# One weight array for the first two products of an encoder layer, and transposes four half steps later

## The chip, the cores and the metric

The kernel runs on one core of a Trainium2 chip. The metric is the device time of one execution in microseconds (us). The core has five engines that run side by side, each through its own list of instructions: TensorE (PE, matrix products, results go to PSUM banks), VectorE (DVE), ScalarE (ACT), GpSimd (POOL) and SyncE (SP), which here issues nearly all DMAs.

## The reference, cut to what matters

A trunk of two layers on 256 tokens of width 1024, in float32. The first layer, the even one, has two groups of attention heads behind one input projection:

```python
def even_mixer(xn, w_in, rpb, q_norm, w_uq, kv_norm, w_ukv, w_o, cos_r, sin_r):
    hcat = xn @ w_in                      # 1024 x (3*512 + 256 + 128 + 32)
    a_qkv = hcat[..., :o0]                # queries, keys, values of neighbourhood attention
    out_a = neighbourhood_attention(...)
    c_q = rms_norm(hcat[..., o0:o1], q_norm)      # latent inputs: 256
    c_kv = rms_norm(hcat[..., o1:o2], kv_norm)    # and 128 columns,
    k_pe = apply_rope(hcat[..., o2:], ...)        # and 32 columns
    q = (c_q @ w_uq) ...; kv = (c_kv @ w_ukv) ...
    out_b = dense_attention(q, k, v, ...)
    return jnp.concatenate([out_a, out_b], axis=-1) @ w_o
```

`xn` is the RMS norm of `x`. After each mixer comes an MLP, then the odd layer, its MLP, and a final norm.

## The kernel before, in words

Activations lie feature first: `x` is 8 tiles of 128 features by 256 tokens. Precision is kept by splitting each operand of a product into a rounded upper part and the rest: a weight tile `raw` becomes `whi` (ACT, a cast, line 167) and `wlo` (DVE, a subtraction, line 168), `x` becomes `xh` and `xl` (`prepare`), and each product is three matmuls (`mm3`, lines 171 to 173: upper by upper, then the two cross terms).

Weights are loaded in the order of the list `specs` into four raw buffers, and split in four pieces each (`split_piece`). `weight()` hands out the next split weight and first issues loads and splits some weights ahead.

The even layer starts with two products that have the tokens as rows: the latent inputs, 416 columns from `w_c` (banks `pc`, one for each half of the tokens), and the values, 512 columns from `w_v` (`pv`). Before the change `c_product` runs inside the loop over the 8 tiles of `x`; the values follow behind it (`v_steps`), with `rstd(s)` (the norm's factor: two small matmuls at line 223, DVE at 225, POOL at 231) among them. The norm's factor is applied to results, not to `x`: `c_tail` (lines 487 to 508) squares and normalizes the latent inputs in 2 + 1 parts with ACT, POOL and DVE in turn, rotates 32 columns (`kpe`), and returns a step that transposes the result on PE (line 506) and splits it into `cT`; `v_out` scales the values.

Then come queries and keys of neighbourhood attention, four weights `w_qk` of two heads each. `qk_steps(c)` gives four half steps of 12 matmuls; its last multiplies the result by `both` (the norm's factor as a row, made by `as_row`, line 258) into `q32`, and splits that into `qk_h` and `qk_l`. From the second weight on these half steps form the list `main`, into which the attention's steps (`side`: scores at line 180, transposes of probabilities, mixing) are woven by their costs; the first scores need `qk_h` and `qk_l` of the first weight.

Inside `manual_schedule` the three engines keep the written order. Elsewhere a scheduler orders the instructions when the program is built; each engine then runs its list in that order, and an instruction that waits for a semaphore holds up all behind it on its engine. `issue_after` keeps a block's instructions behind a given one.

Of the kernel before, what the change touches and what calls it, by code (L numbers as in the profile page):

```python
# [20 lines left out]
ENG = mybir.EngineType  # L21
# [9 lines left out]
NEG = -1e30  # L31
EPS = 1e-6

MLA_SCALE = (64 + 32) ** -0.5
WCH = 2048
WBUFS = 3
# [8 lines left out]
def trunk(ctx, tc, a, out):  # L45
# [23 lines left out]
    def bank(tag):  # L69
        return ps.tile([P, 512], F32, tag=tag, name=tag)  # L70
# [28 lines left out]
    def plan(name, n):  # L99
        for j in range(a[name].shape[0]):  # L100
            specs.append((a[name][j], n))
# [7 lines left out]
        for j in (14, 15):  # L109
            specs.append((a["w2"][layer, j], WCH))  # L110

    plan("w_c", 4 * 416)
    plan("w_v", 4 * 512)
    plan("w_qk", WCH)
    plan("w_ukv", 1024)
    plan("w_uq", 2 * 768)
# [12 lines left out]
    def load_weight(pieces=1, before=lambda i: None):  # L129
        j = state["loaded"]  # L130
        src, n = specs[j]
        raw = wraw.tile([P, WCH], F32, tag="raw", name="raw")
        for i in range(pieces):
            c = cut(j, i, pieces)
            before(i)
            nc.sync.dma_start(raw[:, c], src[:, c])
        parts[j] = [raw, None, None]
        state["loaded"] = j + 1
# [31 lines left out]
    def mm3(o, sh, sl, mh, ml, first, last):  # L170
        nc.tensor.matmul(o, sh, mh, start=first, stop=False)  # L171
        nc.tensor.matmul(o, sh, ml, start=False, stop=False)  # L172
        nc.tensor.matmul(o, sl, mh, start=False, stop=last)  # L173
# [17 lines left out]
    def tok(t):  # L191
        return slice(t * P, (t + 1) * P)
# [254 lines left out]

    def even(ep):
        xT = xh, xl = half_tile(act, "xh", 2), half_tile(act, "xl", 2)
        for j in range(2):  # L450
            load_weight(4, lambda i: nc.sync.dma_start(x[:, 4 * j + i, :], a["x"][:, 4 * j + i, :]))
        load_weight(2)
        load_weight()
        both = ep.tile([P, 2, T], F32, name="both")

        cosr = ep.tile([P, NT, 32], F32, name="cosr")
# [22 lines left out]
        kpe = ep.tile([P, NT, 32], F32, name="kpe")  # L479
        vna = ep.tile([P, NT, 512], F32, name="vna")  # L480

        def c_product(pc, wc, k, t):
            wh, wl = wc
            ws = slice((k % 4) * 416, (k % 4) * 416 + 416)
            mm3(pc[:, 0:416], xh[:, k, tok(t)], xl[:, k, tok(t)], wh[:, ws], wl[:, ws], k == 0, k == KT - 1)

        def c_tail(t, pc):
            rt = column(r, t)
# [18 lines left out]
                split(cT_h[:, 0:3, tok(t)], cT_l[:, 0:3, tok(t)], pt[:, 0:384].rearrange("p (k n) -> p k n", k=3))  # L507
            return step

        def v_steps(t):  # L510
            hold = []

            def step(ks):
                if not hold:
                    hold.append(bank("acc"))
                for k in ks:
                    if t == 0 and k % 4 == 0:
                        wv.append(weight())
                    wh, wl = wv[k // 4]
                    ws = slice((k % 4) * 512, (k % 4) * 512 + 512)  # L520
                    mm3(hold[0], xh[:, k, tok(t)], xl[:, k, tok(t)], wh[:, ws], wl[:, ws], k == 0, k == KT - 1)
                return hold[0]
            return step

        def v_out(t, pv):
            nc.scalar.activation(vna[:, t, :], pv, AF.Copy, scale=column(r, t))

        wc, wv = [], []
        pc = [bank("acc") for _ in range(NT)]
        s = sum_tile()  # L530
        with tc.manual_schedule(engines={ENG.PE, ENG.Activation, ENG.DVE}):
            for k in range(KT):
                upper, lower = prepare(k, 0, xT)
                upper()
                lower()
                split_piece()
                if k % 4 == 0:
                    wc.append(parts[k // 4][1:])
                for t in range(NT):
                    c_product(pc[t], wc[k // 4], k, t)  # L540
                if k % 2:
                    add_squares(k // 2, s)
            state["used"] = 2
            del parts[0], parts[1]
            ins = [split_piece() for _ in range(WPARTS)][-1]
        with tc.issue_after(ins[0]), tc.issue_after(ins[1]):
            with tc.manual_schedule(engines={ENG.PE, ENG.Activation, ENG.DVE}):
                v0, v1 = v_steps(0), v_steps(1)
                v0(range(4))
                small_loads()  # L550
                r = rstd(s)
                dg = [diagonal(r, t) for t in range(NT)]
                v1(range(4))
                pv = v0(range(4, KT))
                turn_c = [c_tail(0, pc[0])]
                v_out(0, pv)
                turn_c.append(c_tail(1, pc[1]))
                v_out(1, v1(range(4, KT)))


        qk = {}
# [157 lines left out]
        nc.scalar.mul(both[:, 0, :], row, HD ** -0.5)  # L719
        nc.scalar.copy(both[:, 1, :], row)  # L720
        run_all(first[3:])
        turn_c[0]()


        accs, wo = [], {}
        main = [(1.31, f) for c in range(1, 4) for f in qk_steps(c)]
        main.insert(1, (0, turn_c[1]))
        i = lambda t, h: 2 * t + h
        for h in range(2):
            main += [(.65, kg[i(0, h)]), (.98, ug[i(0, h)]), (.43, kt[i(0, h)]), (.65, kg[i(1, h)]), (.43, ut[i(0, h)]),  # L730
# [219 lines left out]
def _layout(i):  # L950
    f = np.ascontiguousarray
    w = i["ev_w_in"][0]
    d = {"x": f(i["x"][0][ORDER].T.reshape(KT, P, T).transpose(1, 0, 2))}
    d["w_c"] = f(w[:, 1536:].reshape(2, 4, P, 416).transpose(0, 2, 1, 3).reshape(2, P, -1))
    d["w_qk"] = f(w[:, :1024].reshape(KT, P, 2, 4, P).transpose(3, 1, 0, 2, 4).reshape(4, P, -1))
    d["w_v"] = f(w[:, 1024:1536].reshape(2, 4, P, 512).transpose(0, 2, 1, 3).reshape(2, P, -1))
    d["w_uq"] = f(i["ev_w_uq"][0].reshape(1, 2, P, 768).transpose(0, 2, 1, 3).reshape(1, P, -1))
    d["w_ukv"] = f(i["ev_w_ukv"][0].reshape(1, P, 1024))
    d["w_oe"] = f(i["ev_w_o"][0].reshape(4, 2, P, D).transpose(0, 2, 1, 3).reshape(4, P, -1))
# [44 lines left out]
```

## Time and profile before

| what | value |
|---|---|
| median of 3 runs | 767.98 us (767.9 to 768.18) |
| the profiled execution's own time | 768.55 us |
| its span, first to last instruction | 766.7 us |
| PE busy | 757.2 us, 99% of the span |
| DVE, ACT busy | 500.8 us (65%), 507.5 us (66%) |

A matmul's record shows its start and a modelled end; matmuls overlap, so the distance from start to start is what one costs on PE. A row of the timeline gives start, duration, engine, line, operation, what it writes and reads, how many records are merged, and in brackets how long its engine was idle before it and what ended that.

### The profile page before, as it was taken

What the parts mean: (1) busy time and instruction counts of PE and PEld (TensorE: products, weight loads), DVE (VectorE), ACT (ScalarE), POOL (GpSimd) and SP (SyncE); (2) the same over time, 40 slices, a digit from 0 to 9 for tenths busy, and PEclk for the clock granted to TensorE, in tenths of its full rate; (3) what the DMA queues carried; (4) which work ended last, traced back from release to release, by engine and by line L of the source; (5) the groups of instructions that cost most, each with busy time, mean ns of one, the idle gap of its engine ahead of it and who ended that gap; (6) DMA issues with size and microseconds to landing.
All of it is one profiled execution on the core that took longest, in us unless ns stands there. A gap on an engine that the chain in (4) does not pass through costs nothing.

```text
span 766.7 us, 14611 instructions
## 1 busy us (share of the span) xinstructions
PE 757.2 (99%) x5898; PEld 716.6 (93%) x5898; DVE 500.8 (65%) x1028; ACT 507.5 (66%) x1078; POOL 9.5 (1%) x22
## 2 busy tenths in 40 slices
PE   8999999999999999999999999999999999999996
PEld 5998999999999999999999999999999899899895
DVE  6788858655555557877667676767749555555564
ACT  6788967444444445888988989989857454454541
POOL 0100000000000001000000000000000000000000
PEclk9999999999999999999999999999999999999999
DMA  8763334555555444643452534435454554554501
GB/s 282 302 227 132 111 110 167 173 212 167 172 212 168 170 186 149 207 160 125 167 183 104 203 110 176 159 120 184 165 194 164 172 214 165 172 213 168 178 40 55
DMA packets 22819, 129.13 MB, mean 168 GB/s; under 512 B 2913, under 2 KB 5473, under 8 KB 9825
## 3 DMA queue, kind: packets, MB, share of 16 engines
q1 hardware_dynamic: 22464, 127.94, 47.5%
q8 instruction: 46, 0.75, 0.4%
q10 hardware_dynamic: 288, 0.28, 0.1%
q14 instruction: 21, 0.16, 0.1%
HBM read 127.16 MB, written 1.05 MB: 167 GB/s over the span
## 4 chain that ended last, share of the span: by engine, by line
PE 89%; ACT 5%; DVE 2%; issue 2%; DMA 1%; SPq 0%; POOLq 0%; POOL 0%
PE acc L171 19%; PE acc L172 18%; PE acc L173 18%; PE w L171 9%; PE w L172 9%; PE w L173 9%; PE w L180 1%; DMA raw<-in_w_c 1%; ACT whi L167 1%; PE w L859 1%; PE w L683 1%; PE w L843 1%; PE w L697 1%; DVE wlo L168 1%; PE acc L868 1%
## 5 line engine op out<-in xcount | busy, mean ns | idle before, releaser
L168 DVE TENSOR_TENSOR wlo<-raw,whi 128x512 fp32r<-128x512 f32 (+3 forms) x488 | 307.5, 663 | 165.6 <-ACT whi L167 164.6
L167 ACT CAST whi<-raw 128x512 fp32r<-128x512 f32 (+3 forms) x488 | 268.7, 600 | 201.9 <-issue 173.3
L172 PE MATMUL w<-xl,whi 128*128 128x256 f32 x528 | 149.1, 282 | 0.0
L173 PE MATMUL w<-xh,wlo 128*128 128x256 f32 x528 | 149.0, 282 | 0.0
L171 PE MATMUL w<-xh,whi 128*128 128x256 f32 x528 | 148.8, 282 | 0.0
L171 PE MATMUL acc<-xh,whi 128*128 128x256 f32 x432 | 125.2, 290 | 0.0
L173 PE MATMUL acc<-xh,wlo 128*128 128x256 f32 x432 | 121.9, 282 | 0.0
L172 PE MATMUL acc<-xl,whi 128*128 128x256 f32 x432 | 121.8, 282 | 0.0
L171 PEld LDWEIGHTS w<-xh,whi 128*128 128x128 f32 x528 | 99.6, 189 | 0.6
L172 PEld LDWEIGHTS w<-xl,whi 128*128 128x128 f32 x528 | 99.3, 188 | 0.5
L173 PEld LDWEIGHTS w<-xh,wlo 128*128 128x128 f32 x528 | 99.5, 188 | 0.0
L171 PEld LDWEIGHTS acc<-xh,whi 128*128 128x128 f32 x432 | 81.4, 188 | 2.4 <-issue 1.4
L172 PEld LDWEIGHTS acc<-xl,whi 128*128 128x128 f32 x432 | 81.6, 189 | 0.0
L173 PEld LDWEIGHTS acc<-xh,wlo 128*128 128x128 f32 x432 | 81.2, 188 | 0.0
L171 PE MATMUL acc<-hh,whi 128*128 128x256 f32 x256 | 72.6, 284 | 0.0
L172 PE MATMUL acc<-hl,whi 128*128 128x256 f32 x256 | 72.4, 283 | 0.0
L173 PE MATMUL acc<-hh,wlo 128*128 128x256 f32 x256 | 72.4, 283 | 0.0
L171 PE MATMUL acc<-whi,xh 128*128 128x384 f32 (+2 forms) x160 | 57.5, 359 | 0.9 <-ACT whi L167 0.9
L172 PE MATMUL acc<-wlo,xh 128*128 128x384 f32 (+2 forms) x160 | 55.8, 349 | 0.4 <-DVE wlo L168 0.4
L173 PE MATMUL acc<-whi,xl 128*128 128x384 f32 (+2 forms) x160 | 54.9, 343 | 0.0
L171 PEld LDWEIGHTS acc<-hh,whi 128*128 128x128 f32 x256 | 49.1, 192 | 0.0
L173 PEld LDWEIGHTS acc<-hh,wlo 128*128 128x128 f32 x256 | 49.1, 192 | 0.0
(202 smaller groups left out, 1289.9 us busy)
## 6 DMA issues: line engine op xcount, KB each, us to landing
raw<-in_w SPq DMA_DIRECT2D x64, 1024.0 KB, 4.8
raw<-in_w_oqk SPq DMA_DIRECT2D x24, 1024.0 KB, 4.8
raw<-in_w_ov SPq DMA_DIRECT2D x16, 768.0 KB, 4.3
raw<-in_w_qk SPq DMA_DIRECT2D x4, 1024.0 KB, 10.5
raw<-in_w_oe SPq DMA_DIRECT2D x4, 1024.0 KB, 5.2
raw<-in_w_oo SPq DMA_DIRECT2D x4, 1024.0 KB, 4.8
bias<-in_rpb SPq DMA_DIRECT2D x8, 256.0 KB, 4.0
raw<-in_w_c SPq DMA_DIRECT2D x8, 208.0 KB, 4.7
```

Source lines behind the costliest of these rows:

```text
L167: a = nc.scalar.copy(hi, src).ins
L168: return a, (eng or nc.vector).tensor_tensor(lo, src, hi.bitcast(F32), op=ALU.subtract).ins
L171: nc.tensor.matmul(o, sh, mh, start=first, stop=False)
L172: nc.tensor.matmul(o, sh, ml, start=False, stop=False)
L173: nc.tensor.matmul(o, sl, mh, start=False, stop=last)
L180: nc.tensor.matmul(o[j], y[pb, 0, ts], z[pb, 1, :], start=n == 0, stop=n == 2)
L683: nc.tensor.transpose(pt[:, b * P:(b + 1) * P], pp[:, b // 2, (b % 2) * P:(b % 2 + 1) * P], ident)
L697: nc.tensor.matmul(pvo[64 * j:64 * j + 64, 0:P], v[:, kk, h * 64:(h + 1) * 64], pts[:, 2 * j + kk, :], start=kk == 0, stop=kk == NT - 1)
L843: nc.tensor.matmul(ss[j][rows, T:T + P], d["q12"][:, j, i * P + 64 * c:i * P + 64 * c + 64], d["k12"][:, j, 2 * i + c, :], start=True, sto ...
L859: nc.tensor.transpose(pt[:, b * P:(b + 1) * P], pp[:, b * P:(b + 1) * P], ident)
L868: nc.tensor.matmul(pvo[cs, 0:P], d["v0"][:, kk, cs], turned[i, j][:, kk, :], start=kk == 0, stop=False)
```

## The change

`w_c` and `w_v` become one array, `w_cv`, with 416 + 512 columns for each tile of 128 features; a raw buffer holds two tiles' worth (1856 columns). It is loaded in pieces: the first buffer in four of 464 columns (with the first two tiles of `x` between them), the other three in two pieces of 928 columns, each behind its tile of `x`. As each tile of `x` arrives, both products are done with it, for both halves of the tokens: 6 matmuls of 416 and 6 of 512 columns. `rstd`, `c_tail` and `v_out` stand behind all of them, and the split of the next weight (`w_qk`, first of four) stands in the program behind those. The two transposing steps `turn_c`, before run after the first weight's half steps and one half step later, stand behind the four half steps of the second weight.

```diff
-    plan("w_c", 4 * 416)
-    plan("w_v", 4 * 512)
+    plan("w_cv", 2 * CV)
...
-        for j in range(2):
-            load_weight(4, lambda i: nc.sync.dma_start(x[:, 4 * j + i, :], a["x"][:, 4 * j + i, :]))
+        def load_x(k):
+            nc.sync.dma_start(x[:, k, :], a["x"][:, k, :])
+
+        load_weight(4, lambda i: load_x(i // 2) if i % 2 == 0 else None)
+        for j in range(1, 4):
+            load_weight(2, lambda i: load_x(2 * j + i))
         load_weight(2)
-        load_weight()
...
-        def c_product(pc, wc, k, t):
-            wh, wl = wc
-            ws = slice((k % 4) * 416, (k % 4) * 416 + 416)
-            mm3(pc[:, 0:416], xh[:, k, tok(t)], xl[:, k, tok(t)], wh[:, ws], wl[:, ws], k == 0, k == KT - 1)
+        def first_products(o, w, k, t, c0, n):
+            ws = slice((k % 2) * CV + c0, (k % 2) * CV + c0 + n)
+            mm3(o[:, 0:n], xh[:, k, tok(t)], xl[:, k, tok(t)], w[0][:, ws], w[1][:, ws], k == 0, k == KT - 1)
...
-        wc, wv = [], []
-        pc = [bank("acc") for _ in range(NT)]
+        pc, pv = [bank("acc") for _ in range(NT)], [bank("acc") for _ in range(NT)]
         s = sum_tile()
         with tc.manual_schedule(engines={ENG.PE, ENG.Activation, ENG.DVE}):
             for k in range(KT):
                 upper, lower = prepare(k, 0, xT)
                 upper()
                 lower()
-                split_piece()
-                if k % 4 == 0:
-                    wc.append(parts[k // 4][1:])
+                for _ in range(WPARTS // 2):
+                    ins = split_piece()
+                w = parts[k // 2][1:]
                 for t in range(NT):
-                    c_product(pc[t], wc[k // 4], k, t)
+                    first_products(pc[t], w, k, t, 0, 416)
+                for t in range(NT):
+                    first_products(pv[t], w, k, t, 416, 512)
                 if k % 2:
                     add_squares(k // 2, s)
-            state["used"] = 2
-            del parts[0], parts[1]
-            ins = [split_piece() for _ in range(WPARTS)][-1]
+                    state["used"] += 1
+                    del parts[k // 2]
         with tc.issue_after(ins[0]), tc.issue_after(ins[1]):
-            with tc.manual_schedule(engines={ENG.PE, ENG.Activation, ENG.DVE}):
-                v0, v1 = v_steps(0), v_steps(1)
-                v0(range(4))
-                small_loads()
-                r = rstd(s)
-                dg = [diagonal(r, t) for t in range(NT)]
-                v1(range(4))
-                pv = v0(range(4, KT))
-                turn_c = [c_tail(0, pc[0])]
-                v_out(0, pv)
-                turn_c.append(c_tail(1, pc[1]))
-                v_out(1, v1(range(4, KT)))
+            small_loads()
+            r = rstd(s)
+            dg = [diagonal(r, t) for t in range(NT)]
+            turn_c = [c_tail(t, pc[t]) for t in range(NT)]
+            for t in range(NT):
+                v_out(t, pv[t])
...
         run_all(first[3:])
-        turn_c[0]()
...
         main = [(1.31, f) for c in range(1, 4) for f in qk_steps(c)]
-        main.insert(1, (0, turn_c[1]))
+        main[4:4] = [(0, f) for f in turn_c]
```

ScalarE, from the end of the last square of `x` on, before. `whi` is a weight's upper part, `junk` belongs to `c_tail` (a square with its sum), `vna` is `v_out`.

```order
L213 ACTIVATE q<-x 128x512
L167 CAST whi<-raw 128x512 x12
L494 ACTIVATE junk,ss<-acc,rstd 128x256
L167 CAST whi<-raw 128x512 x4
L494 ACTIVATE junk,ss<-acc,rstd 128x128
L526 ACTIVATE vna<-acc,rstd 128x512
L494 ACTIVATE junk,ss<-acc,rstd 128x256
L167 CAST whi<-raw 128x512 x2
L494 ACTIVATE junk,ss<-acc,rstd 128x128
```

The twelve casts are the two value weights and the first `w_qk`, the four behind the first square are the second `w_qk`. The same place of the changed kernel (its lines are shifted by two):

```order
L213 ACTIVATE q<-x 128x512
L167 CAST whi<-raw 128x512 x4
L496 ACTIVATE junk,ss<-acc,rstd 128x256
L513 ACTIVATE vna<-acc,rstd 128x512 x2
L496 ACTIVATE junk,ss<-acc,rstd 128x128
L167 CAST whi<-raw 128x512 x4
L496 ACTIVATE junk,ss<-acc,rstd 128x256
L700 ACTIVATE both<-w 128x256
L701 COPY both<-w 128x256
L167 CAST whi<-raw 128x512 x4
L496 ACTIVATE junk,ss<-acc,rstd 128x128
L167 CAST whi<-raw 128x512 x4
```

Only the first `w_qk` is still split ahead of `c_tail`; the second, third and fourth now stand among and behind its squares.

VectorE, the instructions ahead of the first `q` (the product with `both` of which `qk_h` and `qk_l` are made), before:

```order
L498 SCALAR_TENSOR_TENSOR cn<-acc,rstd,gc 128x256
L168 TENSOR_TENSOR wlo<-raw,whi 128x512 x2
L495 TENSOR_SCALAR ss<-ss 128x1
L497 TENSOR_TENSOR rstd<-rstd 128x1
L498 SCALAR_TENSOR_TENSOR cn<-acc,rstd,gc 128x128
L500 TENSOR_SCALAR kp<-acc,rstd 128x32
L470 TENSOR_TENSOR r_371<-kp,cosr 128x32
L472 TENSOR_TENSOR r_372<-kp,sinr 128x16 x2
L576 TENSOR_TENSOR q_466<-w,both 128x512
```

And in the changed kernel:

```order
L500 SCALAR_TENSOR_TENSOR cn<-acc,rstd,gc 128x256
L168 TENSOR_TENSOR wlo<-raw,whi 128x512 x2
L497 TENSOR_SCALAR ss<-ss 128x1
L168 TENSOR_TENSOR wlo<-raw,whi 128x512
L499 TENSOR_TENSOR rstd<-rstd 128x1
L168 TENSOR_TENSOR wlo<-raw,whi 128x512
L500 SCALAR_TENSOR_TENSOR cn<-acc,rstd,gc 128x128
L502 TENSOR_SCALAR kp<-acc,rstd 128x32
L168 TENSOR_TENSOR wlo<-raw,whi 128x512
L473 TENSOR_TENSOR r_366<-kp,cosr 128x32
L475 TENSOR_TENSOR r_367<-kp,sinr 128x16 x2
L557 TENSOR_TENSOR q_463<-w,both 128x512
```

This is the second half of the tokens. Between the first half's `kp` (the last that `c_tail` reads from its bank) and this `q` the changed kernel has ten subtractions `wlo`, five of them in these rows: all of the second and third `w_qk` and two of the fourth. Before, there were two in that stretch, of the third `w_qk`; the four of the second stood among the first half's `c_tail`.

TensorE at the first scores, changed kernel (`L180` are the scores of the first two heads, `L508` the transposes of both `turn_c`):

```order
L171 MATMUL acc<-xh,whi 128x256
L172 MATMUL acc<-xl,whi 128x256
L180 MATMUL w<-qk_h 128x256 x2
L508 MATMUL w<-ident,cn 128x128 x6
L173 MATMUL acc<-xh,wlo 128x256
L180 MATMUL w<-qk_l,qk_h 128x256 x2
L180 MATMUL w<-qk_h,qk_l 128x256 x2
```

Before, the transposes stood in two groups of three, ahead of and one half step into the second `w_qk`, and all six scores stood together behind that weight's 48 matmuls; now the scores stand 8 matmuls into the third weight, with the six transposes between them.

## Rows read from the trace of the kernel before

**Rows 1.** The page's first part: busy time, share, instructions; matmuls, then weight loads.

```profile
PE 757.2 (99%) x5898; PEld 716.6 (93%) x5898; DVE 500.8 (65%) x1028; ACT 507.5 (66%) x1078; POOL 9.5 (1%) x22
```

**Rows 2.** Windows: stretch, its length, five engines' busy time, granted clock, DMA share, GB/s.

```profile
4.70:17.00 12.30, 11.18 (x50) 8.89 (x49) 9.72 (x21) 9.38 (x20) 0.00 (x0) 1.00 0.95 317
```

**Rows 3.** Timeline of PE, 1 to 10 us: warm-up matmuls, first latent products.

```profile
1.19 3.59 PE L81 MATMUL acc<-warm 128*128 128x512 bf16 x8 [1.19 <-DVE warm L76]
...
4.72 0.71 PE L171 MATMUL acc<-whi,xh 128*128 128x416 f32 x1
...
6.29 0.34 PE L173 MATMUL acc<-whi,xl 128*128 128x416 f32 x1
...
7.59 0.45 PE L171 MATMUL acc<-whi,xh 128*128 128x416 f32 x1 [0.95 <-ACT whi L167]
...
8.51 0.36 PE L173 MATMUL acc<-whi,xl 128*128 128x416 f32 x1
...
9.26 0.35 PE L171 MATMUL acc<-whi,xh 128*128 128x416 f32 x1
```

**Rows 4.** Timeline of ACT, 4 to 22 us: casts of weights as they land.

```profile
4.14 0.52 ACT L167 CAST whi<-raw 128x416 fp32r<-128x416 f32 x1
...
7.00 0.54 ACT L167 CAST whi<-raw 128x416 fp32r<-128x416 f32 x1 [1.85 <-DMA raw<-in_w_c]
...
14.46 0.54 ACT L167 CAST whi<-raw 128x416 fp32r<-128x416 f32 x1 [0.75 <-DMA raw<-in_w_c]
...
15.72 2.42 ACT L167 CAST whi<-raw 128x512 fp32r<-128x512 f32 x4 [0.19 <-DMA raw<-in_w_v]
...
19.58 2.18 ACT L167 CAST whi<-raw 128x512 fp32r<-128x512 f32 x4 [1.43 <-DMA raw<-in_w_v]
```

**Rows 5.** Timeline of PE, 20 to 42 us: norm, values' end, queries' start, first scores.

```profile
20.06 0.50 PE L223 MATMUL w<-mean,squares 128*128 128x1 f32 x4
...
20.42 0.48 PE L171 MATMUL acc<-whi,xh 128*128 128x512 f32 x1
...
27.75 0.39 PE L172 MATMUL acc<-wlo,xh 128*128 128x512 f32 x1
...
28.93 0.28 PE L171 MATMUL w<-xh,whi 128*128 128x256 f32 x1
...
29.05 0.28 PE L172 MATMUL w<-xl,whi 128*128 128x256 f32 x1
...
41.63 0.39 PE L180 MATMUL w<-qk_h 64*128 64x256 f32 x2
```

**Rows 6.** Timeline, 22 to 24 us: the norm's factor, on DVE and POOL.

```profile
22.65 0.15 DVE L225 TENSOR_SCALAR ms<-w 128x2 f32<-128x2 f32 x1
...
22.95 0.71 POOL L231 TENSOR_TENSOR rstd<-ms,mhalf 128x2 f32<-128x2 f32 x1 [21.51 <-DVE ms L225]
```

**Rows 7.** Timeline of ACT and DVE, 24 to 38 us: `c_tail`, then `q` and `qk_h`.

```profile
24.16 0.47 ACT L494 ACTIVATE junk<-acc,rstd 128x256 f32<-128x256 f32 x1
...
32.46 0.15 DVE L495 TENSOR_SCALAR ss<-ss 128x1 f32<-128x1 f32 x1
...
33.26 0.16 DVE L497 TENSOR_TENSOR rstd<-rstd 128x1 f32<-128x1 f32 x1 [0.65 <-POOL rstd L198]
...
33.86 1.28 DVE L168 TENSOR_TENSOR wlo<-raw,whi 128x512 fp32r<-128x512 f32 x2
...
33.97 0.37 ACT L494 ACTIVATE junk<-acc,rstd 128x128 f32<-128x128 f32 x1 [1.91 <-DVE cn L498]
...
35.06 0.15 DVE L495 TENSOR_SCALAR ss<-ss 128x1 f32<-128x1 f32 x1
...
36.60 0.19 DVE L470 TENSOR_TENSOR r<-kp,cosr 128x32 f32<-128x32 f32 x1
...
36.88 0.68 DVE L576 TENSOR_TENSOR q<-w,both 128x512 f32<-128x512 f32 x1
...
37.59 0.62 ACT L167 CAST qk_h<-q 128x512 fp32r<-128x512 f32 x1
```

More of the change, by code (lines that the diff above doesn't have):

```diff
@@ L32 @@
 EPS = 1e-6
+CV = 416 + 512
 MLA_SCALE = (64 + 32) ** -0.5
@@ L508, in c_tail @@
             return step
[L510 to L523, printed above, removed]
         def v_out(t, pv):
             nc.scalar.activation(vna[:, t, :], pv, AF.Copy, scale=column(r, t))
-        wc, wv = [], []
-        pc = [bank("acc") for _ in range(NT)]
+        pc, pv = [bank("acc") for _ in range(NT)], [bank("acc") for _ in range(NT)]
         s = sum_tile()
@@ L953, in _layout @@
     d = {"x": f(i["x"][0][ORDER].T.reshape(KT, P, T).transpose(1, 0, 2))}
-    d["w_c"] = f(w[:, 1536:].reshape(2, 4, P, 416).transpose(0, 2, 1, 3).reshape(2, P, -1))
+    d["w_cv"] = f(np.concatenate([w[:, 1536:], w[:, 1024:1536]], 1).reshape(4, 2, P, CV).transpose(0, 2, 1, 3).reshape(4, P, -1))
     d["w_qk"] = f(w[:, :1024].reshape(KT, P, 2, 4, P).transpose(3, 1, 0, 2, 4).reshape(4, P, -1))
-    d["w_v"] = f(w[:, 1024:1536].reshape(2, 4, P, 512).transpose(0, 2, 1, 3).reshape(2, P, -1))
     d["w_uq"] = f(i["ev_w_uq"][0].reshape(1, 2, P, 768).transpose(0, 2, 1, 3).reshape(1, P, -1))
```

## Prediction, made before the changed kernel ran

> **What bounds the kernel now.** I read the page first: PE is busy 99% of the span, weight loads 93% [rows 1], so a change counts by what it does to the moments when PE waits. The windows at the program's start show the one stretch that the change can shorten: from 4.7 to 17 us PE is busy for 11.18 of 12.30 us, while the DMA engines are busy for 95% [rows 2]. The reader should see there a PE that is fed by arrivals. The timelines of PE and ACT say how: after the first tile's six matmuls, begun at 4.72, the next begins at 7.59, 0.59 us after the cast that had waited 1.85 us for its weights [rows 3, 4]. The last piece of `w_c` is cast at 14.46, also after a wait for a DMA, and only then come the values, whose weights were waited for again, at 15.72 and 19.58 [rows 4]. The values end and the queries begin at 28.93 [rows 5]. Last I followed the chain from the norm's factor through `c_tail` to `q`, `qk_h` and the first scores at 41.63 [rows 5 to 7], since the change moves its start. PE is busy 757.2 of the 766.7 us [rows 1], and 3.5 of the 9.5 idle ones lie, as the next part shows, before 28.93: behind that there is little idle time in which a gain or a delay could vanish, so what is won or lost by 45 us stays to the end.
>
> **Term A: the products.** What PE must do from 4.72 to 28.93 is 48 matmuls of 416 columns, 48 of 512, and the norm's matmuls. The first cost 0.1875 us each (four steps, 8.51 to 9.26) [rows 3], so 9.00 us. The second cost 0.236 (five steps, 27.75 to 28.93), so 11.33; line 223 takes 20.42 - 20.06 = 0.36 [rows 5]. Together 20.69 of 24.21 us: 3.52 us are waits.
>
> After the change the work is the same, 2.54 us for each tile of `x` instead of 1.13, and arrivals need to keep up with PE only at the beginning. Four waits remain:
> - The first tile's start, as before: 4.72 to 6.29 for five steps [rows 3] is 0.63 over.
> - Its values need the second piece of 464 columns. With 128 partitions of 4 bytes a tile of `x` is 128 KB and such a piece 232 KB, so x and two pieces are 592 KB. Before, 336 KB (one tile and one piece) had landed by 4.14, and 672 KB at 7.00 [rows 4]. In proportion 592 KB land at 6.32, and PE starts 0.59 later, at 6.91, where it is free at 6.48: 0.43.
> - The `wlo` of that piece follows one subtraction later: 7.59 to 8.51 for two matmuls [rows 3], 0.92 against 0.47, so 0.45.
> - The second tile's first piece makes 960 KB; 1008 KB were there in time for 9.26 [rows 3]. PE comes to it at about 8.8, so between 0 and 0.9; I take 0.3.
>
> Sum 1.81. Later tiles arrive in time if DMA delivers as before: the fifth needs 5 x 592 = 2960 KB, which lie between 2688 KB (14.46) and 3200 (15.72) [rows 4], hence at 15.13, plus 0.6 for the cast and 0.6 for the subtraction 16.3; PE reaches it at 4.72 + 1.81 + 4 x 2.54 = 16.7. The eighth needs the 4736 KB that were there at 19.58 [rows 4], and PE reaches it at 24.3. The queries thus begin at 4.72 + 20.69 + 1.81 = 27.22 instead of 28.93: **A = -1.7**. Bounds: waits of 1.1 (the second piece is there on time) give -2.4; waits as long as now give 0.
>
> DVE and ACT had 9.72 and 9.38 us of work from 4.7 to 17 [rows 2], or 1.2 for each of 8 tiles; each tile now brings one more piece to cast and subtract, at most 0.61 (a fourth of 2.42) [rows 4] and 0.64 (half of 1.28) [rows 7]. That is 1.9 us a tile against PE's 2.54, so they are hidden; with PE's waits gone they would be the next limit, 0.6 us a tile away. The first `w_qk` lands 1024 KB after 19.58; 3200 to 4736 KB took 3.86 us [rows 4], hence at 22.2, and is split by 25, with 2 us in hand before 27.2. The small loads and the POOL instructions pass nothing that waits for them earlier.
>
> The Trainium skill, DMA: Bandwidth & Descriptors, Rules for kernel authors, wants 128 partitions and at least 1 MiB per DMA for full bandwidth. The new loads of 464 KB beside pieces of 208 KB are nearer to that, and by the rule A would go to its -2.4 and the sum below to 0.1. I keep to the old arrivals.
>
> **Term B: what stands behind the products.** The norm's matmuls, before at 20.06 among the values [rows 5], now stand behind them all, at 27.22 - 0.36 = 26.86, and with them `rstd`, `c_tail` and, in ACT's queue behind `c_tail`'s squares, the splits of the second to fourth `w_qk`. The rows of the order show ten subtractions between the first half's `kp` and `q`. So the chain to the first scores has to run from 26.86:
> - line 223 takes 0.50 [rows 5], DVE's `ms` to the start of POOL 0.30, POOL 0.71 [rows 6]: 28.4.
> - the first square 0.47 [rows 7] and about 0.1 to read its sum: 29.0.
> - from `ss` to the second square, through POOL and `cn`, 32.46 to 33.97 [rows 7], 1.51; that square and its sum 0.37 + 0.1: 31.0.
> - from `ss` to the end of `kp`, 35.06 to 36.60 [rows 7], 1.54: 32.5. Until here DVE has nothing else, because the casts that would feed it stand behind that second square.
> - then DVE is full: ten subtractions at 0.60 (33.86 to 35.06 holds two) are 6.0; the second half's `c_tail` is 1.51 + 1.54 less two waits for POOL of 0.65 [rows 7], which the subtractions now fill, 1.75; the rotation twice 0.28 (36.60 to 36.88), 0.56; its last addition 0.1. Sum 8.4: `q` starts at 40.9.
> - `q` to the cast of `qk_h` 0.71, that cast 0.62 [rows 7]: 42.25. The scores can start at 42.3.
>
> PE comes to them after 104 matmuls of 0.12 (28.93 to 29.05) [rows 5], 12.5, and `as_row`, about 0.4: before, 28.93 to 41.63 held 96 such matmuls (11.5), `as_row` and two groups of transposes, so these three share 1.2. That is 27.22 + 12.9 = 40.1. **PE waits 2.2 us at the first scores**, where before `qk_h` was ready 3.4 us early (38.21 against 41.63). Behind the waiting scores stand the six transposes, whose inputs are ready, and the third `w_qk`: all of PE. The second pair of scores waits for `qk_l` perhaps 0.1 longer, and dividing the scores around the transposes costs PE two more changes of shape, taken as 0.1 each: several such changes fit into the 1.2 above. **B = +2.5**. B hangs on the norm and moves with it, so an earlier end of the products does not shorten it. Bounds: 1.8 (each of some 20 DVE instructions 0.03 shorter) to 3.2 (as much longer).
>
> The later place of the transposes alone costs nothing: the matmuls that read `cT` come after two more weights, over 8 us later, and their number is the same.
>
> **Sum.** -1.7 + 2.5 = +0.8 us. On the profiled execution (span 766.7, own time 768.55) that gives 767.5 and 769.35. The median is 0.57 below that execution, so I forecast **768.8 us**, with 767.4 (both bounds below, -2.4 + 1.8) to 769.9 as its own range. A difference under about 0.2%, 1.5 us, can't be told from no change here; the forecast is no change.
>
> **Rivals.**
> - *Slower: arrivals set the pace of the products.* Each tile now needs 592 KB before PE can finish it, where it needed 336. If the fifth tile comes 1.5 us after its place in the old curve, or the second piece at 7.0 and the fifth tile 0.7 late, A is no better than -0.7 and the sum passes +1.8. With A = 0 it is +2.5: 770.5. For it: 95% DMA share already [rows 2], and only 0.4 us in hand at the fifth tile. Against it: 4 us in hand at the last tile, and fewer, larger transfers. 0.17.
> - *Faster: the chain to the scores is hidden.* If DVE reaches `q` two us earlier than I add up, because the subtractions find gaps before 32.5 or the scores find other work ahead of them, B is nearly gone and A stands alone: -1.7, 766.3. It decides from B under 0.2. For it: before, the same chain had 3.4 us in hand. Against it: an engine's list is fixed, and ACT's shows the casts behind the squares. 0.10.
> - *Slower: the clock.* The eight warm-up matmuls took 3.59 us [rows 3], 0.44 each for 512 columns against 0.236 later: the level of 1.2 GHz, then 2.4. From 4.7 to 17, with a wait of about 1.1 us in it, the granted clock is 1.00 [rows 2]. If the new wait at the scores let it fall, and it took as long as the warm-up to rise, half of 3.59 would be lost, +1.8 on top of +0.8: 770.6. The Trainium skill, TensorE: Matmul & The Clock Gate, Part 1: The HAM clock gate, says that the slow level is the default and that sustained work releases it, so a long enough idle time brings it back; no wait here before shows one. 0.03.
>
> **How the numbers follow.** Forecast 0.70, rivals 0.17, 0.10 and 0.03. The forecast's own tails cross 1.5 us hardly: same 0.70, slower 0.20, faster 0.10. The bounds of A and B together give 767.4 on one side and 771.2 (0 + 3.2) on the other. The range 766.9 to 770.2 holds the forecast's own range and reaches towards 766.3 and 770.5; outside are most of the faster case and the far half of the slower ones, some 2 in 10.
>
> **What the profile of the changed kernel would show.** The first matmul of the queries at 27.2 (25.5 to 28); line 223 just before it; a wait of PE of about 2.2 us at line 180 near 40 to 42 us, ended by the cast of `qk_h`; VectorE without a gap for the 8 us before `q`, and idle before 27. I am wrong if PE waits for casts of `w_cv` after 10 us, if the scores start without a wait, or if the queries begin before 26 or after 28.5.

## The result and the profile after

The changed kernel is slower: a median of 771.44 us (771.03 to 772.21, 4 runs) beside 768.08 us (767.9 to 768.29, 4 runs) for the kernel before. The ratio is 1.0045, its 95% interval 1.0027 to 1.0062. The forecast was 768.8 us, no change, with a range to 770.2: it was wrong by 2.6 us, and the time lies outside the range.

The page of the changed kernel has the sum almost as before [rows 1]; but the row PEclk of its second part, the granted clock in 40 slices, has an 8 in the third slice:

```profile
PE 758.9 (99%) x5898; PEld 719.2 (93%) x5898; DVE 501.0 (65%) x1028; ACT 507.7 (66%) x1078; POOL 9.9 (1%) x22
...
PEclk9989999999999999999999999999999999999999
```

The windows of the changed kernel take that slice apart (stretch, length, busy time of PE, PEld, DVE, ACT and POOL, granted clock, DMA share, GB/s); the first answers to [rows 2]:

```profile
4.70:17.00 12.30, 11.94 (x53) 9.89 (x54) 10.17 (x19) 10.42 (x23) 0.00 (x0) 1.00 0.99 357
...
39.80:42.00 2.20, 0.00 (x0) 0.00 (x0) 2.20 (x9) 0.28 (x1) 0.00 (x0) 0.94 0.83 320
42.00:44.00 2.00, 1.61 (x7) 1.39 (x8) 2.00 (x4) 1.73 (x5) 0.00 (x0) 0.50 0.40 160
44.00:48.00 4.00, 4.00 (x20) 3.55 (x19) 2.61 (x9) 2.93 (x9) 0.00 (x0) 0.50 0.67 229
48.00:49.00 1.00, 1.00 (x9) 0.86 (x9) 0.00 (x0) 0.18 (x1) 0.00 (x0) 0.72 0.89 344
49.00:52.00 3.00, 3.00 (x29) 2.57 (x27) 2.19 (x9) 1.64 (x6) 0.00 (x0) 1.00 0.24 82
```

From 4.7 to 17 us PE now works 11.94 of 12.30 us instead of 11.18: the products are no longer starved. But from 39.8 PE does nothing for over 2 us, and towards the end of that its clock goes to half, 1.2 GHz. Counting back from 0.94 (0.06 x 2.20 / 0.5 = 0.26) and 0.72 (0.28 / 0.5 = 0.56), it is at half from 41.74 to 48.56. Before, it never left 1.00 in this part of the program.

PE's timeline after, which answers to [rows 3, 5]:

```profile
4.84 0.46 PE L171 MATMUL acc<-whi,xh 128*128 128x416 f32 x1 [0.29 <-ACT whi L167]
...
6.56 0.39 PE L171 MATMUL acc<-whi,xh 128*128 128x512 f32 x1
...
26.25 0.50 PE L223 MATMUL w<-mean,squares 128*128 128x1 f32 x4
26.61 0.37 PE L171 MATMUL w<-xh,whi 128*128 128x256 f32 x1
...
39.52 0.28 PE L172 MATMUL acc<-xl,whi 128*128 128x256 f32 x1
42.39 0.58 PE L180 MATMUL w<-qk_h 64*128 64x256 f32 x2 [2.59 <-ACT qk_h L167]
...
45.69 0.41 PE L172 MATMUL acc<-xl,whi 128*128 128x256 f32 x1
45.90 0.41 PE L173 MATMUL acc<-xh,wlo 128*128 128x256 f32 x1
...
48.73 0.39 PE L180 MATMUL w<-qk_h 64*128 64x256 f32 x2
```

The queries begin at 26.61, 2.3 us before those of the profiled execution of before. Then 2.59 us are lost at the first scores, and behind them a matmul of 256 columns costs 0.21 us (45.69 to 45.90) where it cost 0.12. The chain that ends the wait, on VectorE and ScalarE, answers to [rows 6, 7]:

```profile
26.79 0.16 DVE L225 TENSOR_SCALAR ms<-w 128x2 f32<-128x2 f32 x1 [3.10 <-PE w L223]
...
32.02 0.24 DVE L502 TENSOR_SCALAR kp<-acc,rstd 128x32 f32<-128x32 f32 x1
32.17 0.68 DVE L168 TENSOR_TENSOR wlo<-raw,whi 128x512 fp32r<-128x512 f32 x1
...
35.53 0.16 DVE L499 TENSOR_TENSOR rstd<-rstd 128x1 f32<-128x1 f32 x1 [0.43 <-POOL rstd L198]
...
38.99 0.16 DVE L499 TENSOR_TENSOR rstd<-rstd 128x1 f32<-128x1 f32 x1 [0.43 <-POOL rstd L198]
...
41.00 0.68 DVE L557 TENSOR_TENSOR q<-w,both 128x512 f32<-128x512 f32 x1
...
41.72 0.62 ACT L167 CAST qk_h<-q 128x512 fp32r<-128x512 f32 x1 [2.16 <-DVE q L557]
```

VectorE stands still for 3.10 us until the norm's matmuls come. Up to the end of the first half's `kp` it still waits between the steps of the chain; from the first subtraction behind it, at 32.17, it works without a gap but for two of 0.43 us: `q` at 41.00, `qk_h` from 41.72, the scores at 42.39. The forecast had 40.9 and 42.3. So everything that the prediction said the profile would show is there, but for those two gaps; the clock was not on its list.

So the first theory: the products give 2.3 us, the wait at the scores takes 2.6, and the half clock that follows some 3 more. Its rivals: the loss is the wait alone, and the clock's stretch hides behind VectorE, which is late too; the loss comes from the moved transposes or the new weight array; the clock falls for another reason than the wait.

### The profile page after: what moved, and what is told of

It reads as the page before. It is cut to its first block, busy times and chain, and to the rows that moved or that the text cites. A ratio compares the mean times of both kernels' runs of the same rounds, so it can differ in the third digit from the quotient of the medians.

```text
span 770.2 us, 14611 instructions
## 1 busy us (share of the span) xinstructions
PE 758.9 (99%) x5898; PEld 719.2 (93%) x5898; DVE 501.0 (65%) x1028; ACT 507.7 (66%) x1078; POOL 9.9 (1%) x22
## 4 chain that ended last, share of the span: by engine, by line
PE 89%; ACT 5%; DVE 3%; issue 2%; POOL 1%; DMA 0%; POOLq 0%; SPq 0%; DVEq 0%
PE acc L171 19%; PE acc L172 18%; PE acc L173 18%; PE w L171 8%; PE w L172 8%; PE w L173 8%; PE w L180 2%; DVE wlo L168 1%; ACT whi L167 1%; PE w L839 1%; PE w L664 1%; PE w L823 1%; PE w L678 1%; PE acc L848 1%; ACT sw L793 1%
## 5 line engine op out<-in xcount | busy, mean ns | idle before, releaser
L172 PEld LDWEIGHTS acc<-hl,whi 128*128 128x128 f32 x256 | 49.1, 192 | 0.0
```

## The experiments

Each median is of 4 to 11 executions, its ratio is to 15 to 27 executions of the kernel before on the same chip.

### A busy PE in the wait: fill and fill_half

```diff
+        def fill(n):
+            o = bank("acc")
+            for _ in range(n):
+                with tc.high_priority(NORM_PRIO):
+                    tc.keep_in_program_order(nc.tensor.matmul(o, warm[:, 0:P], warm, start=True, stop=True))
...
+                    if (c, f, k) == (2, 0, 1):
+                        fill(13)
```

(6 in fill_half.)

> The changed kernel with 13 matmuls of zeros (bf16, 512 columns, into a bank of their own) just ahead of the first scores, where PE waited 2.59 us; two matmuls of the third w_qk stand behind the scores now. Theory (the wait let the granted clock fall, and the slow stretch of 6.8 us cost about 3.1 us): PE is busy up to 42.4, the granted clock stays at 1.00, 256 columns stay at 0.12, the scores start at 42.4 as before, and the time is 768.3 (767.8 to 768.8). Rival (the fall has another cause than PE's wait, the transfers or the moved transposes): the clock falls all the same, 771.4. Rival (the clock costs nothing, the wait alone the whole): clock at 1.00, time 771.4.

> As fill, with 6 matmuls of zeros instead of 13, which leaves a wait of some 1.5 us (1.2 to 1.8) behind them. The scores start at 42.4 in every theory. If a wait of this length lets the clock fall too: a stretch at 1.2 GHz of about 6.8 us and 771.4. If it is too short for that: the clock at 1.00 and 768.3. The longest wait of PE in the kernel before, 0.9 us, brought no fall; the 2.59 us of the changed kernel did.

fill: 770.84 us, ratio 1.0035 (1.0022 to 1.0048). fill_half: 770.34 us, 1.0034 (1.0022 to 1.0047). The timeline of fill:

```profile
39.21 2.98 PE L548 MATMUL acc<-warm 128*128 128x512 bf16 x12
42.19 0.39 PE L180 MATMUL w<-qk_h 64*128 64x256 f32 x2
43.44 0.39 PE L180 MATMUL w<-qk_l,qk_h 64*128 64x256 f32 x2 [0.86 <-DVE qk_l L168]
```

(One of the 13 matmuls of zeros has no record.) The clock stayed at 1.00 in fill, as the theory said, but the time fell by 0.6 us, not 3.1. The scheduler had also put the transposes behind all the scores, so PE now waited 0.86 us for `qk_l`, which the transposes cover in the changed kernel. In fill_half the profiled execution, the slowest at 772.08, waited 1.51 and 0.86 us and its clock was at half from about 43.8 to 47.2 (windows of fill_half):

```profile
42.00:44.00 2.00, 0.43 (x4) 0.23 (x4) 2.00 (x6) 1.90 (x5) 0.00 (x0) 0.95 0.46 193
44.00:46.00 2.00, 2.00 (x11) 1.78 (x11) 1.79 (x6) 0.64 (x3) 0.00 (x0) 0.50 0.15 20
46.00:48.00 2.00, 2.00 (x15) 2.00 (x14) 1.77 (x6) 2.00 (x8) 0.00 (x0) 0.69 0.91 369
```

Its mean clock was 0.996; the other four took 770.03 to 770.51 at 0.998 or 0.999. One kernel, with a fall and without: 1.8 us apart, but by one execution against four. Both readings stayed open.

### The wait without the rest of the change: hold_pe and norm_late

hold_pe is the kernel before with a matmul of zeros ahead of the first scores that waits for GpSimd; norm_late is the kernel before with the later transposes and with the norm and both tails behind all value products.

```diff
+            for _ in range(18):
+                tc.keep_in_program_order(nc.gpsimd.tensor_tensor(table, mean[:, 0:1], mhalf, op=ALU.pow))
+            tc.keep_in_program_order(nc.gpsimd.memset(late, 0.0))
+            first = tc.keep_in_program_order(nc.tensor.matmul(o, late, warm, start=True, stop=True))
+            held.enter_context(tc.issue_after(first.ins))
```

And norm_late:

```diff
                 v0(range(4))
-                small_loads()
-                r = rstd(s)
-                dg = [diagonal(r, t) for t in range(NT)]
                 v1(range(4))
...
+                pv = [v0(range(4, KT)), v1(range(4, KT))]
+                small_loads()
+                r = rstd(s)
+                dg = [diagonal(r, t) for t in range(NT)]
+            turn_c = [c_tail(t, pc[t]) for t in range(NT)]
```

> The kernel before with one matmul of zeros ahead of the first scores, whose operand GpSimd finishes late (18 small operations behind its last rstd at 35.8, 0.4 to 0.54 us each, so at 43 to 45.6), and with the rest of PE's list behind it: a wait of 2 to 4.5 us and nothing else of the change. Theory: the clock falls some 2 us into the wait, and the time rises by the wait plus about 3 us: 768.1 + 3.3 + 3.1 = 774.5 (772.5 to 776). Rival (a wait costs its own length): the wait alone, 770 to 772.6, with the clock at 1.00.

> The kernel before, with its own weight arrays, the transposes four half steps later, and the norm's matmuls, rstd, the diagonals and the tails behind all value products: the second part of the change without the first. Theory (the later norm makes the wait): the chain through VectorE ends later than PE comes to the first scores, a wait of 1 to 2 us there for qk_h; 768.2 + 1.4 = 769.6 if the clock stays, up to 772 if it falls. Rival (the loss lies in the new weight array): no wait, 768.

hold_pe: 777.39 us, ratio 1.0119 (1.0105 to 1.0133). The GpSimd operations took longer than I had taken, and the wait was 6.87 us; of the 9.4 us lost, 2.5 are not the wait. The clock was at half from inside the wait (0.81 in the window of 42 to 44) to about 53.5 (0.63 in that of 52 to 54). norm_late: 771.79 us, 1.004 (1.0028 to 1.0052), with the old weight arrays. Its scores:

```profile
43.79 0.38 PE L180 MATMUL w<-qk_h 64*128 64x256 f32 x2 [1.95 <-ACT qk_h L167]
```

And a window behind them:

```profile
44.00:48.00 4.00, 4.00 (x21) 3.35 (x20) 3.44 (x11) 2.62 (x9) 0.00 (x0) 0.57 0.51 202
```

Two executions took 770.4 us at a mean clock of 0.999, three 771.8 to 772.0 at 0.996 or 0.997. The scores themselves still ran at full clock; the fall came behind the wait. The later norm, with the tails behind it, is enough for the wait; the weight array isn't needed for the loss.

### The parts: turn_old and before_turn_late

turn_old is the changed kernel with `turn_c` at its old places; before_turn_late is the same edit the other way round, in the kernel before.

```diff
         run_all(first[3:])
+        turn_c[0]()
...
-        main[4:4] = [(0, f) for f in turn_c]
+        main.insert(1, (0, turn_c[1]))
```

> The changed kernel with the transposes of the latents at their old places, so the weight array and the order of the products alone. Theory: the late norm holds these transposes too; PE waits for cn some 1.5 us near 36 us and 0.6 us near 39, and comes to the scores when qk_h is ready, without a wait. The same 2 us are lost, in two pieces: 768.7 if the clock stays at 1.00, 771 if it falls. Rival (the moved transposes are the loss): 766.

> The kernel before with the transposes alone moved four half steps later. Theory: qk_h was ready 3.4 us early, so PE comes to the scores 1 us earlier and still waits for nothing; the transposes follow behind them: 768.0 (767.6 to 768.4). Rival (the later transposes make the loss): 770 or more.

turn_old: 770.39 us, ratio 1.0033 (1.0021 to 1.0044); before_turn_late: 768.27 us, 1.0005 (0.9996 to 1.0014). The transposes cost nothing by themselves that is clear of the noise, as forecast. Where they stay, they take over the wait (timeline of turn_old):

```profile
37.61 0.41 PE L508 MATMUL w<-ident,cn 128*128 128x128 f32 x2 [2.03 <-DVE cn L500]
...
40.70 0.33 PE L508 MATMUL w<-ident,cn 128*128 128x128 f32 x1 [0.65 <-DVE cn L500]
```

The time was 1.7 us above what I had expected; the waits were 2.7 us instead of 2.1, and what else was lost there I did not follow. The clock, which the expectation left open, did not fall in the profiled execution, though its first wait is longer than that of norm_late (windows of turn_old; the first holds the end of that wait):

```profile
36.00:38.00 2.00, 0.39 (x4) 0.42 (x5) 1.70 (x5) 1.50 (x6) 0.26 (x1) 1.00 0.55 123
38.00:42.00 4.00, 3.35 (x29) 3.15 (x28) 3.56 (x13) 2.50 (x5) 0.92 (x1) 1.00 0.48 162
```

before_turn_late also showed something that the forecast had missed. Its program begins as that of before does, yet its queries began 0.85 us earlier than in [rows 5], and the second tile's first product at 6.97 instead of 7.59 [rows 3]:

```profile
6.97 0.34 PE L171 MATMUL acc<-whi,xh 128*128 128x416 f32 x1
...
28.08 0.28 PE L171 MATMUL w<-xh,whi 128*128 128x256 f32 x1
```

### A shorter chain: norm_early, q_first, latents_first, latents_turn6

norm_early puts the norm between the last tile's latent and value products; q_first puts the splits of later weights behind `q`; latents_first does the latent products of the last two tiles ahead of their value products, with the norm between; latents_turn6 has the transposes two half steps later still. The core of latents_first:

```diff
+                if k == KT - 1:
+                    small_loads()
+                    r = rstd(s)
+                    dg = [diagonal(r, t) for t in range(NT)]
+                for j in [k] if k < KT - 2 else range(KT - 2, KT) if k == KT - 1 else []:
+                    for t in range(NT):
+                        first_products(pv[t], w, j, t, 416, 512)
```

norm_early has the same lines for the norm without the change of the loop over `j` (in both the last sums of squares, which the norm needs, stand ahead of those values too), latents_turn6 has `main[6:6]` for `main[4:4]` besides, and the core of q_first is:

```diff
-                    hold["w"], hold["p"] = weight(), bank("acc" if c else "w")
+                    with tc.issue_after(q_ins[0]) if c else ExitStack():
+                        hold["w"] = weight()
```

> The changed kernel with the norm's matmuls, rstd, the diagonals and the small loads between the last tile's latent products and its value products instead of behind them. Theory (the chain from the norm to qk_h makes the wait): the chain starts 1.4 us earlier, the norm's matmuls at 25.2, and in the order that results the scores stand some 28 matmuls earlier on PE with waits of about 0.6 and 0.4 us, too short for the clock to fall: 767 (766 to 768). Rival (the loss lies in the products or the transposes, not in this chain): 771.

> The changed kernel with the splits of the third and later w_qk behind the first q on VectorE (some six subtractions fewer ahead of it). The order that results has the first scores 8 matmuls earlier on PE. Theory: the wait is the chain's through VectorE; qk_h is ready at about 40, PE waits some 1.1 us at the scores and 0.9 us at their second group, together 0.5 us less than the 2.59 of the changed kernel. If two waits of 1 us keep the clock at 1.00: 768.3; if it falls for part of the runs: 768.3 to 770.9. Rival (the ten subtractions don't matter): 771.4.

> The changed kernel with the latent products of the last two tiles of x ahead of their value products, and the norm's matmuls, rstd, the diagonals and the small loads between them, so that the chain to the first scores starts 2.8 us earlier than in the changed kernel. Theory (the wait at the first scores is the whole loss, in its own length and in the clock that it lets fall): no wait of PE at the scores over 0.3 us, the clock at 1.00, PE's lead of 2.2 us of the products kept but for 0.5 to 1.2 us: 766.9 (766.2 to 767.5). Rival (something else in the products or the transposes costs the time): 768 or more.

> As latents_first, with the transposes six half steps later instead of four. Theory: nothing waits at the scores; the transposes stand where they part no scores from their softmax, 0.2 us less than latents_first: 767.1 (766.7 to 767.5), the fastest of these kernels. Rival (the later transposes hold up what reads the latents): 767.5 or more.

| kernel | median us | ratio to before, 95% | PE's waits at the first scores |
|---|---|---|---|
| norm_early | 768.08 | 1.0005 (0.9996 to 1.0014) | 0.56 (for `qk_l`) |
| q_first | 769.57 | 1.0026 (1.0017 to 1.0035) | 1.11 and 0.87 |
| latents_first | 767.35 | 0.9992 (0.9983 to 1.0001) | none |
| latents_turn6 | 767.21 | 0.9989 (0.998 to 0.9997) | none |

Each start of the chain that comes earlier takes away wait and time together, and latents_turn6 is 0.8 us faster than the kernel before, with an interval that ends just below 1 (timeline: the norm at 23.60, the queries 3.2 us behind it, the scores without a wait):

```profile
23.60 0.50 PE L223 MATMUL w<-mean,squares 128*128 128x1 f32 x4
...
26.84 0.28 PE L171 MATMUL w<-xh,whi 128*128 128x256 f32 x1
...
38.89 0.39 PE L180 MATMUL w<-qk_h 64*128 64x256 f32 x2
```

q_first's executions spread from 768.93 to 771.72: four took 770.3 us or more at a mean clock of 0.995 or 0.996, six at most 769.8 at 0.997 or 0.998, among them the profiled one, whose clock did not fall at the scores. So two waits of about 1 us, close together, seem to have cost the clock in some executions; no profile shows one of these. All of norm_early, latents_first and latents_turn6 were expected 0.1 to 1.1 us faster than they were.

### The clock alone: fill_turn, after_again, fill_kept, fill_kept5, after_kept

fill_turn is fill with the transposes back between the two groups of scores; after_again is the changed kernel itself.

```diff
+            if n == 1:
+                run_all(between)
...
-                two_heads(sb, *qk[hp], tok(t))
+                two_heads(sb, *qk[hp], tok(t), turn_c if n == 0 else ())
```

> The changed kernel with 13 matmuls of zeros ahead of the first scores, as in fill, and with the transposes between the two groups of those scores, where the changed kernel has them, so that PE does not wait for qk_l, which cost fill 0.86 us. Then it is the changed kernel with a PE that is busy instead of waiting, and the clock is all that differs. Theory: granted clock 1.00 throughout, no wait at the scores, and 771.4 less the 1.3 to 2.7 us by which executions with a fall exceeded those without in q_first and fill_half: 769.4 (768.7 to 770.1). Rival (the wait is the loss and the clock adds nothing): 771.4.

> The changed kernel once more, on the same chip and beside the same runs as fill_turn: 771.4 (770.8 to 772.2), the mean granted clock 0.995 to 0.997, a wait of 2.4 to 2.9 us at the first scores and a fall of the clock in it. If the wait is at the edge of what brings a fall, some executions are without one, at 769 to 770 with a mean clock of 0.998 or more.

fill_turn: 771.47 us, ratio 1.0044 (1.0032 to 1.0056), with the clock at 1.00. after_again: 771.11 us, 1.0044 (1.0028 to 1.006); five executions at a mean clock of 0.995 to 0.997 and 770.92 to 774.0 us, one at 0.998 and 769.63. The first says that the clock costs nothing, the second that it costs about 1.3 us or more. But in fill_turn the scheduler, which counts the zeros as work, had reordered VectorE too: the first `rz`, the reciprocal in the softmax, begins at 48.98 us in its timeline and at 47.07 in that of the changed kernel, and PE's second scores wait for a subtraction and take 0.85 us for 0.39:

```profile
47.01 0.85 PE L182 MATMUL w<-qk_h 64*128 64x256 f32 x2 [0.17 <-DVE cl L168]
```

So the last three keep the changed kernel's order, instruction by instruction, on PE, VectorE and ScalarE (`KEEP` lists it), and add nothing, 11 or 5 matmuls of zeros:

```diff
+            seq = [traced[f"I-{k + j}"] for k, m in runs for j in range(m) if f"I-{k + j}" in traced]
+            if eng == "PE":
+                at = [z.name for z in seq].index("I-538")
+                seq[at:at] = zeros
+            for k, m in zip(seq, seq[1:]):
+                tc.add_manual_dep(m, k.name, mybir.DependencyInfo(mybir.DependencyClass.NoSync, mybir.DependencyReason.DATA),
+                                  reason="kept order")
```

> The changed kernel with 11 matmuls of zeros directly ahead of the first scores, and with the order of the changed kernel kept on TensorE, VectorE and ScalarE up to the end of the layer's attention, so that nothing but PE's activity in the wait differs (fill and fill_turn also had VectorE in another order). The zeros take 2.5 us and end before qk_h is there. Theory of the clock: granted clock 1.00, and the time falls from 771.1 by what executions with a fall exceeded those without in after_again, norm_late and fill_half (1.3 to 1.8 us): 769.6 (769.0 to 770.2). Rival (VectorE is as late as PE, and a PE at full clock only waits later): 771.1, with new waits of PE at the second scores or at the transposes of pp.

> As fill_kept with 5 matmuls of zeros, which leaves a wait of 1.4 us in one piece (fill_half's was 1.51 and 0.86). If the fall hangs on how long PE is without work: fewer executions fall, the mean clock is 0.998 or more in most, and the time is near that of fill_kept; those that fall are 1.3 to 1.8 us above. If it doesn't: all fall, 771.1.

> The control: the changed kernel with its own order written out in the same way and no zeros, instruction for instruction the changed kernel. 771.2 (770.8 to 771.9), the clock falling in the wait in most executions (mean 0.995 to 0.997).

| kernel | median us | ratio to before, 95% | wait at the first scores |
|---|---|---|---|
| after_kept | 771.38 | 1.0047 (1.0035 to 1.006) | 2.60 |
| fill_kept | 769.65 | 1.0023 (1.0014 to 1.0031) | 0.21 |
| fill_kept5 | 769.60 | 1.0025 (1.0016 to 1.0034) | 1.50 |

The first matmul of the queries, the first and second scores, the first matmul of the output projection behind the attention (`acc<-oah,whi`), and two windows, of after_kept:

```profile
26.73 0.37 PE L176 MATMUL w<-xh,whi 128*128 128x256 f32 x1
...
42.52 0.38 PE L185 MATMUL w<-qk_h 64*128 64x256 f32 x2 [2.60 <-ACT qk_h L172]
...
44.77 0.41 PE L178 MATMUL acc<-xh,wlo 128*128 128x256 f32 x1
44.99 0.41 PE L176 MATMUL acc<-xh,whi 128*128 128x256 f32 x1
...
47.68 0.39 PE L185 MATMUL w<-qk_h 64*128 64x256 f32 x2
...
80.81 0.28 PE L176 MATMUL acc<-oah,whi 128*128 128x256 f32 x1
```

```profile
42.00:44.00 2.00, 1.48 (x13) 1.21 (x13) 2.00 (x4) 1.93 (x5) 0.00 (x0) 1.00 0.41 172
44.00:48.00 4.00, 4.00 (x23) 3.64 (x23) 2.65 (x9) 2.84 (x9) 0.00 (x0) 0.57 0.62 219
```

And of fill_kept:

```profile
26.63 0.37 PE L176 MATMUL w<-xh,whi 128*128 128x256 f32 x1
...
39.66 2.55 PE L553 MATMUL acc<-warm 128*128 128x512 bf16 x11
42.42 0.38 PE L185 MATMUL w<-qk_h 64*128 64x256 f32 x2 [0.21 <-ACT qk_h L172]
...
46.09 0.39 PE L185 MATMUL w<-qk_h 64*128 64x256 f32 x2
...
79.21 0.28 PE L176 MATMUL acc<-oah,whi 128*128 128x256 f32 x1
```

```profile
44.00:48.00 4.00, 4.00 (x36) 3.63 (x33) 3.81 (x15) 3.25 (x12) 0.00 (x0) 1.00 0.63 240
```

The scores begin at the same time, within 0.1 us. From the first to the second it is 5.16 us with the fall and 3.67 without: 1.5 us, in a stretch where nothing waits and only the clock differs. The fall comes behind the wait here: the scores that end it run at full clock, the window up to 44 has 1.00. The 1.5 us are still there at the output projection, 54.08 us behind the first matmul of the queries in after_kept and 52.58 in fill_kept. The medians differ by 1.73 us. The kernel before takes 49.47 us for that same stretch, from 28.93 [rows 5] to its own row:

```profile
78.40 0.28 PE L171 MATMUL acc<-oah,whi 128*128 128x256 f32 x1
```

In fill_kept5 the wait was 1.50 us (its first scores); the clock stayed at 1.00 to 54 us in its profile, and its median is that of fill_kept:

```profile
42.17 0.39 PE L185 MATMUL w<-qk_h 64*128 64x256 f32 x2 [1.50 <-ACT qk_h L172]
```

This settles it against the rival that VectorE's lateness takes the clock's cost in any case. A shorter wait in the same place spared the clock; but the length does not decide alone, since the profiled executions differ the other way: turn_old kept its clock in a wait of 2.03 us and norm_late lost it with one of 1.95. What else decides stays open. Nor does the mean clock of an execution tell of a fall at the scores by itself: the profiled execution of fill_kept5 has 0.997, and so have some of the kernel before. fill_turn's contrary result is put down to its other order of VectorE; that was read from its trace and not tried by itself.

## Why the prediction was wrong, point by point

- **Term A, the products: right, near in size.** Forecast -1.7, queries at 27.22 for 28.93. The two profiled executions differ by 2.3 us, but single executions vary here. Four traces with the start of before have the queries at 28.93, 28.08, 28.38 and 28.09 (median 28.24), ten with the changed start at 26.36 to 27.38 (median 26.74): **-1.5 us**. So 27.22 was half a microsecond too late, and the 28.93 from which I worked 0.7 later than its like; that the two nearly cancel is luck. The second piece of weights, forecast to land at 6.32 us, was there for the values at 6.56, right behind the latent products, and all waits of PE in the profiled execution came to 1.08 us (26.61 - 4.84 less the 20.69 of work), not 1.81. The rival that arrivals set the pace was wrong. By the rule of the Trainium skill, DMA: Bandwidth & Descriptors, Rules for kernel authors, A would have been -2.4 (an estimate); DMA moved 357 GB/s from 4.7 to 17 us for 317 before [rows 2], and the -1.5 is nearer to my -1.7.
- **The transposes: right.** 768.27 beside 767.83 us, inside the interval of no change.
- **Term B, the chain to the first scores: right in place and cause, too small.** Forecast +2.5 (wait of 2.2 and 0.3 for its surroundings), bounds 1.8 to 3.2. The wait was 2.59 and 2.60. Without the clock, the way from the queries to the output projection takes 52.58 us in fill_kept (52.61 in fill_kept5) and 49.47 before (49.44 in before_turn_late): B is **3.1 us**, some 0.5 of them beside the wait. From line 223 to the scores the chain took 16.14 us (42.39 - 26.25) where I had 15.44: 5.92 for 5.64 up to the end of the first half's `kp`, and 8.83 for 8.4 from there to `q`. In that second part the step that fell short is VectorE's: I let the subtractions fill its two waits for POOL in the second half's `c_tail`, 0.65 each. They filled only part: 0.43 is left of each.
- **The sum without the clock:** forecast +0.8, measured +1.8 (769.65 beside 767.86): the forecast was 1 us short, most of it B's, and the time would still have lain in the range.
- **The clock: this step failed.** It stood among the rivals with a chance of 0.03. Its size was right: 1.8 forecast, 1.7 measured, and its time, 770.6, is the nearest of all the cases. Its weight was wrong. I reasoned from a wait of about 1.1 us that left the granted clock at 1.00 [rows 2] to one of 2.2, for which no row stood on either side. In the profiled executions the clock stayed with a wait of 1.50 us and with one of 2.03, and fell with one of 1.95 and with those of 2.6; by time and mean clock, which are weak signs for a single execution, it fell in some three of five with 1.95 and in 14 of 15 with 2.6. The Trainium skill, TensorE: Matmul & The Clock Gate, Part 1, HAM oscillation, describes the mechanism, a wait that brings back the slow level and a cost of half the slow time that follows. The traces agree on the cost (0.57 in 4 us: 3.4 us slow, 1.5 to 1.7 lost); the waits in the Trainium skill's example are of 3 to 5 us, and here shorter ones were enough.
- **The range.** The upper bounds of A and B that the prediction names, 0 and 3.2, give 771.2 without any clock; the range ended at 770.2 and so left out part of what the terms allowed.

Together, from the traces: -1.5 + 3.1 + 1.5 = +3.1. Between the medians it is +3.4. The 0.3 left is not assigned; executions of the changed kernel differ by more, and the profiled one, with 6.8 us at half clock, took 55.24 us from the queries to the output projection where after_kept took 54.08.

## What to carry to other kernels

When a change makes the bound engine wait for a chain where it never waited, price the wait twice: its length, and the clock that it may cost behind it. A change that shortens the work ahead of such a chain and also moves the chain's start behind that work can lose more than it gains. Here moving the start of the chain up again (the last latent products and the norm first) took the whole loss away and left 0.5 to 0.8 us of the gain of 1.5, and filling the wait with work that nobody needs gave back half of the loss. An experiment that adds instructions under a scheduler changes the order of other engines too: keep the order, or the result speaks of both.

## What was not expected of the hardware

- PE's clock fell with waits of 1.95 and 2.6 us, and once with one of 1.51 us that another of 0.86 followed, but not with one of 1.50 alone, and not with one of 2.03 (turn_old). In the profile of the changed kernel the fall came inside the wait (41.74, the scores at 42.39), in those of norm_late and after_kept behind it, while PE was at work again. It stayed at half for 3.4 us in one execution of the changed kernel's program and 6.8 us in another; a matmul of 256 columns costs 0.213 us there and 0.12 at full clock.
- The same start of a program delivers its first weights up to 0.85 us apart in different executions (queries at 28.08 and 28.93), over half of the 1.5 us that term A came to. A term that lies in such a stretch is better taken from several executions.
